# Twelve multiplications of the identity with itself in each token tile of a retention scan

## The chip, the cores and the metric

The kernel runs on one core of one Trainium2 chip. The metric is the device time of one execution, in microseconds (us).

## What is computed

Two layers of a backbone over 1024 latent and 256 context tokens. In each layer four mixers share an input and an output projection; then comes a ConvFFN. The mixer that matters here is the bidirectional retention, four heads of 64 channels, in chunks of 128 tokens:

```python
def step(s_mem, inp):
    qc, kc, vc = inp
    s = jnp.einsum('bhid,bhjd->bhij', qc, kc) * decay_mask
    o = jnp.einsum('bhij,bhjd->bhid', s, vc) + jnp.einsum('bhid,bhde->bhie', qc * q_dec[..., None], s_mem)
    s_new = s_mem * chunk_dec[:, None, None] + jnp.einsum('bhjd,bhje->bhde', kc * k_dec[..., None], vc)
    return s_new, o
```

The kernel folds both directions into one pass: the decay matrix `rD` holds the sum of the forward and the backward mask, and the state of a tile has the forward direction in its upper 64 rows and the backward in its lower 64.

## The kernel before

A layer runs in this order: input projections with the hyena mixer (`hyena`), the projections of mLSTM, retention and RWKV (`mlstm_proj`, `ret_proj`, `rwkv_front`), the retention itself (`retention`), then RWKV and mLSTM interleaved (`rwkv`, `mlstm`, with steps of the next modulation vectors), the output projection (L1042 to L1044 with `wo`), and the FFN. The time goes mostly to the big products of L1042 to L1044.

`retention` (L810) works on token tiles of 128: 10 in layer 0 (8 latent, 2 context) and 8 in layer 1. First it forms all tiles' key-value products (L840, out to `rSS` at L842) and runs the decay over them on GpSimd (L846, L847). Then comes the loop that the change touches, two nested functions:

- `load(t)` transposes q and k of the tile by TensorE (L852, four transposes into one PSUM bank) and copies them out by ScalarE (`rT`, L854); VectorE scales q by the decays (`q2`, L856), TensorE transposes that too (L858), ScalarE copies it out (L860; the trace names this tile rT as well).
- `use(t, ...)` makes the four heads' scores (L866; two heads share a bank, and even and odd heads lie in different halves of the partitions), VectorE multiplies them by the decay matrix into `rS` (L869, two halves), TensorE adds scores times values and decayed q times state (L872 and L873, one pair a head), and ScalarE copies the result over the tile's q (L874).

The loop calls `load(t+1)` before `use(t)`; after each second tile a group norm (L671 to L678) and a store to `yr` (L679) follow.

PSUM has eight banks: until the end of `retention` there are five `bank` and three `dbank`, each handed out in turn; a tile of `dbank` is given again once its last reader is done. `rwkv_front` uses dbanks in front of the scan (L422, read by VectorE at L423). Behind `retention` the function `psum` closes these pools and opens others on the same memory, and the RWKV stage's SBUF tiles take the room of the scan's.

The order of instructions on each engine isn't the program's: the whole kernel is built under a scheduler that simulates the times of the engines and writes each engine's stream in that order (`tile.TileContext(nc,schedule_with_timeline_sim=True)`). So work of neighbouring functions is mixed, and a change in one place can reorder others. Each engine then runs its stream strictly in turn.

Of the kernel before, what the change touches and what calls it, by code (L numbers as in the profile page):

```python
# [135 lines left out]
class Eng:  # L136

    def __init__(s,nc,pool): s.nc=nc; s.e=nc.gpsimd if pool else nc.vector; s.pool=pool
    def tt(s,out,a,b,op): s.e.tensor_tensor(out=out,in0=a,in1=b,op=op)
# [521 lines left out]
def tm(ap,nt):  # L661
    return ap[0:nt*128].rearrange("(t p) c -> p t c",p=128)


def group_norm(K,Y,out_y,nt,sqt,tag="gn",pool=None):

    nc=K.nc
    v=Y[:,0:nt]; h=Y.shape[2]; n=nt*h; th=lambda t: t[:,:n].rearrange("p (t h) -> p t h",h=h)
    q=sqt[:,:n].rearrange("p (t h) d -> p t h d",h=h)
    s,r=[th((pool or K.p_sm).tile([128,n],F32,tag=tag,name="gn_"+i,bufs=2)) for i in "sr"]  # L670
    nc.vector.tensor_reduce(out=s,in_=v,axis=mybir.AxisListType.X,op=ALU.add)  # L671
    nc.vector.tensor_scalar(out=s,in0=s,scalar1=1.0/64,scalar2=None,op0=ALU.mult)
    nc.vector.tensor_tensor(out=v,in0=v,in1=s.unsqueeze(3).to_broadcast([128,nt,h,64]),op=ALU.subtract)
    nc.scalar.activation(out=q,in_=v,func=ACTF.Square)
    nc.vector.tensor_reduce(out=r,in_=q,axis=mybir.AxisListType.X,op=ALU.add)
    nc.scalar.activation(out=r,in_=r,func=ACTF.Sqrt,scale=1.0/64,bias=K.eps5)
    nc.vector.reciprocal(out=r,in_=r)
    (nc.gpsimd if nt==2 else nc.vector).tensor_tensor(out=q,in0=v,in1=r.unsqueeze(3).to_broadcast([128,nt,h,64]),op=ALU.mult)  # L678
    nc.sync.dma_start(out_y,q.rearrange("p t h d -> p t (h d)"))  # L679


def mlstm(K,l,GT,last,side=None):
# [89 lines left out]
    def weights(t):  # L772
        iF,iB=FWT.index(t),BWT.index(t)
        S=p.tile([128,2,4,128],F32,tag="mI" if t%2==0 else "mL",name="S")
        for d in range(2):
            ru=RU[d]
            u_=U3[:,iF] if d==0 else U3[:,iB,::-1]
            nc.gpsimd.tensor_tensor(out=ru[32:40].rearrange("p (h i) -> p h i",h=4),in0=u_.unsqueeze(1).to_broadcast([8,4,128]),in1=C['mbd'][64:72,d].unsqueeze(2).to_broadcast([8,4,128]),op=A.mult)
            vo=VO[:,iF*128:iF*128+128] if d==0 else VOr[:,(9-iB)*128:(9-iB)*128+128]
            b=K.mbank()  # L780
            mm(b,vo,ru,start=True,stop=False)
            mm(b.rearrange("p (h i) -> p h i",h=4),identb,mmaskb[:,d].to_broadcast([128,4,128]),start=False,stop=True)
            act(out=S[:,d].rearrange("p h i -> p (h i)"),in_=b,func=ACTF.Exp)
        return [S[:,d] for d in range(2)]
    SN=weights(0)
# [30 lines left out]
def retention(K,l,last):  # L816
    nc=K.nc; p=K.p_rt; tt=nc.vector.tensor_tensor; act=nc.scalar.activation; mm=nc.tensor.matmul
    A=ALU; D=K.D
    C={n:p.tile(list(K.a['c_'+n].shape),F32,name="c"+n) for n in ('rD','rQD','rKD','rCD','rcos','rsin')}
    for n in C: nc.sync.dma_start(C[n],K.a['c_'+n])  # L820
    Q,KK_,V=[p.tile([128,10,256],F32,name="rqkv%d"%i) for i in range(3)]
    for i,X in enumerate((Q,KK_,V)):
        for t in range(8 if (last and i==0) else 10): nc.sync.dma_start(X[:,t],D['rqkv'][t*128:t*128+128,i*256:i*256+256])
    SS=p.tile([128,10,4,64],F32,name="rSS"); Y=Q.rearrange("p t (h d) -> p t h d",h=4)
    nc.gpsimd.memset(SS[0:64,FWT[0]],0.0); nc.gpsimd.memset(SS[64:128,BWT[0]],0.0)
    hv=lambda ap: ap.rearrange("p (h d) -> p h d",h=4)
    r5=lambda ap: ap.rearrange("p (h o s x) -> p h o s x",h=4,o=2,s=2)
    def rope(t):
        for X in (KK_,Q):
            x=X[:,t]; tmp=p.tile([128,256],F32,tag="rtmp",name="rtmp",bufs=3)  # L830
            for g in range(2):
                nc.gpsimd.tensor_tensor(out=r5(tmp)[:,:,:,g],in0=r5(x)[:,:,:,1-g],in1=C['rsin'][:,t].rearrange("p (o s x) -> p o s x",o=2,s=2)[:,:,g].unsqueeze(1).to_broadcast([128,4,2,16]),op=A.mult)
            tt(out=hv(x),in0=hv(x),in1=C['rcos'][:,t:t+1].to_broadcast([128,4,64]),op=A.mult)
            tt(out=x,in0=x,in1=tmp,op=A.add)
    for t in [8,9]+[0,7,1,6,2,5,3,4]:
        if t<8: rope(t)
        k2=p.tile([128,4,2,64],F32,tag="rq2",name="k2",bufs=4)
        tt(out=k2,in0=hv(KK_[:,t]).unsqueeze(2).to_broadcast([128,4,2,64]),in1=C['rKD'].unsqueeze(3).to_broadcast([128,4,2,64]),op=A.mult)
        b=K.bank()
        for h in range(4): mm(b[:,h*64:h*64+64],k2[:,h].rearrange("p a d -> p (a d)"),V[:,t,h*64:h*64+64],start=True,stop=True)  # L840
        for q,T in ((slice(0,64),FWT),(slice(64,128),BWT)):
            if t!=T[9]: act(out=SS[q,T[T.index(t)+1]].rearrange("p a d -> p (a d)"),in_=b[q,0:256],func=ACTF.Copy)  # L842
    for i in range(1,9):
        for q,T in ((slice(0,64),FWT),(slice(64,128),BWT)):
            cur,nx=T[i],T[i+1]; tmp=p.tile([128,4,64],F32,tag="rtmp",name="rst",bufs=3)
            nc.gpsimd.tensor_tensor(out=tmp[q],in0=SS[q,cur],in1=C['rCD'][q].unsqueeze(2).to_broadcast([64,4,64]),op=A.mult)  # L846
            nc.gpsimd.tensor_tensor(out=SS[q,nx],in0=SS[q,nx],in1=tmp[q],op=A.add)  # L847
    nt=8 if last else 10
    def load(t):
        b=K.bank()  # L850
        for i,X in enumerate((Q,KK_)):
            for f in range(2): nc.tensor.transpose(b[:,(i*2+f)*128:(i*2+f)*128+128],X[:,t,f*128:f*128+128],K.ident)  # L852
        T=p.tile([128,4,128],F32,tag="rT",name="rT",bufs=2)
        act(out=T.rearrange("p a b -> p (a b)"),in_=b,func=ACTF.Copy)  # L854
        q2=p.tile([128,4,2,64],F32,tag="rq2",name="q2",bufs=4)
        tt(out=q2,in0=hv(Q[:,t]).unsqueeze(2).to_broadcast([128,4,2,64]),in1=C['rQD'].unsqueeze(3).to_broadcast([128,4,2,64]),op=A.mult)  # L856
        b=K.bank()
        for h in range(4): nc.tensor.transpose(b[:,h*128:h*128+128],q2[:,h].rearrange("p a d -> p (a d)"),K.ident)  # L858
        T2=p.tile([128,4,128],F32,tag="rT2",name="rT2",bufs=2)
        act(out=T2.rearrange("p a b -> p (a b)"),in_=b,func=ACTF.Copy)  # L860
        return T,T2
    def use(t,T,T2):
        gr=[K.bank(),K.bank()]
        for h in range(4):
            p0=(h%2)*64; f=h//2
            mm(gr[h%2][:,f*128:f*128+128],T[p0:p0+64,2+f],T[p0:p0+64,f],start=True,stop=True)  # L866
        S=p.tile([128,4,128],F32,tag="rS",name="rS",bufs=2)
        Sv=S.rearrange("p (f q) i -> p f q i",q=2); Dv=C['rD'].rearrange("p (f q) i -> p f q i",q=2)
        for q in range(2): tt(out=Sv[:,:,q],in0=gr[q][:,0:256].rearrange("p (f i) -> p f i",f=2),in1=Dv[:,:,q],op=A.mult)  # L869
        b=K.bank()  # L870
        for h in range(4):
            mm(b[:,h*64:h*64+64],S[:,h],V[:,t,h*64:h*64+64],start=True,stop=False)  # L872
            mm(b[:,h*64:h*64+64],T2[:,h],SS[:,t,h],start=False,stop=True)  # L873
        act(out=Y[:,t].rearrange("p a d -> p (a d)"),in_=b[:,0:256],func=ACTF.Copy)  # L874
    nxt=load(0); done=0
    for t in range(nt):
        cur,nxt=nxt,load(t+1) if t+1<nt else None
        use(t,*cur)
        if t%2:
            sl=slice(done,t+1); done=t+1; n=sl.stop-sl.start  # L880
            group_norm(K,Y[:,sl],tm(D['yr'],nt)[:,sl],n,KK_[:,sl].rearrange("p t (h d) -> p (t h) d",h=4),"gnr",p)
# [587 lines left out]
```

## Time and profile before

| what | us |
|---|---|
| median of 3 runs | 4250.28 |
| lowest and highest of them | 4240.55, 4259.92 |
| the profiled execution | 4248.15 |
| its span, first to last instruction | 4246.4 |
| TensorE busy in the span | 3951.2 (93%) |
| VectorE busy | 2537.2 (60%) |
| ScalarE busy | 1413.6 (33%) |
| GpSimd busy | 764.7 (18%) |

The profile is of one execution, with 70484 instructions. PE is TensorE's matmul, PEld its weight load, DVE is VectorE, ACT ScalarE, POOL GpSimd, SP the engine that issues DMAs. The mean granted clock of TensorE was 0.946 of full speed; it has two levels, 1.0 (2.4 GHz) and 0.5 (1.2 GHz). Ends of matmuls are modelled, so a busy TensorE may still be one that waits.

### The profile page before, as it was taken

How to read it: one execution, taken by the hardware profiler on the slowest of the kernel's cores; microseconds unless marked ns; L12 is line 12 of the kernel's file. 1: busy time of each engine (PE TensorE's matmuls, PEld its weight loads, DVE VectorE, ACT ScalarE, POOL GpSimd, SP SyncE). 2: the span in 40 equal slices, each digit the busy share in tenths (PEclk: the TensorE clock that was granted, in tenths of full speed). 3: DMA queues.
4: the chain of work that ended last, by engine and by line, in shares of the span. 5: the costliest groups of instructions: out<-in, count | busy, mean ns of one | idle time of the engine just before them, and what ended most of it. 6: DMA issues, size and time to landing. Idle time of an engine off the chain costs nothing.

```text
span 4246.4 us, 70484 instructions
## 1 busy us (share of the span) xinstructions
PE 3951.2 (93%) x28176; PEld 3225.0 (76%) x28176; DVE 2537.2 (60%) x4756; ACT 1413.6 (33%) x2849; POOL 764.7 (18%) x1538
## 2 busy tenths in 40 slices
PE   5999999799979999999997999997899799999998
PEld 2788887677768888888885678886776678888886
DVE  5755665777669444444448565677767684444447
ACT  4433333554344211111113433344543442212121
POOL 3320023323312000000021221025432220000002
PEclk6999999799989999999998999998898799999999
DMA  4235554344443110111103325554333331111112
GB/s 165 76 96 180 151 156 121 109 149 125 129 147 120 46 40 30 45 40 35 35 30 121 90 87 157 171 162 118 118 115 109 124 111 55 50 40 55 45 50 99
DMA packets 477154, 414.50 MB, mean 98 GB/s; under 512 B 48827, under 2 KB 443284, under 8 KB 474010
## 3 DMA queue, kind: packets, MB, share of 16 engines
q1 hardware_dynamic: 476826, 409.99, 31.1%
q8 instruction: 222, 3.64, 0.3%
q14 instruction: 106, 0.87, 0.1%
HBM read 323.65 MB, written 86.25 MB: 97 GB/s over the span
## 4 chain that ended last, share of the span: by engine, by line
PE 53%; DVE 9%; DMA 4%; issue 2%; ACT 2%; POOL 1%; SPq 1%; DVEq 0%; ACTq 0%; POOLq 0%
PE bank L1043 9%; PE bank L1042 9%; PE bank L1044 9%; PE dbank L1042 6%; PE dbank L1043 6%; PE dbank L1044 6%; DVE bst L1003 1%; DMA xt<-x 1%; DVE facc L1225 1%; PE mbank L993 1%; PE bank L186 1%; DMA adaw<-in_ada_w 1%; PE bank L187 1%; DVE facc L1226 0%; DMA wst<-in_w_out 0%
## 5 line engine op out<-in xcount | busy, mean ns | idle before, releaser
L1042 PE MATMUL dbank<-uh,wh 128*128 128x512 f32 (+1 forms) x2120 | 763.7, 369 | 8.6 <-ACT tmpB L398 5.5
L1043 PE MATMUL dbank<-ul,wh 128*128 128x512 f32 (+1 forms) x2120 | 759.8, 367 | 0.0
L1036 DVE TENSOR_TENSOR wl<-wst,wh 128x1024 fp32r<-128x1024 f32 x146 | 185.9, 1275 | 510.3 <-ACT wh L1035 355.1
L1044 PE MATMUL dbank<-uh,wl 128*128 128x512 f32 (+1 forms) x2120 | 481.5, 367 | 0.0
L1042 PEld LDWEIGHTS dbank<-uh,wh 128*128 128x128 f32 x2120 | 400.6, 189 | 84.0 <-ACT tmpB L398 5.9
L1043 PEld LDWEIGHTS dbank<-ul,wh 128*128 128x128 f32 x2120 | 400.9, 189 | 68.7 <-issue 1.1
L1044 PEld LDWEIGHTS dbank<-uh,wl 128*128 128x128 f32 x2120 | 365.7, 188 | 71.0 <-issue 1.7
L1284 DVE TENSOR_TENSOR facc<-facc,bank 128x512 f32<-128x512 f32 x324 | 221.8, 687 | 205.1 <-PE bank L1044 205.1
L1042 PE MATMUL bank<-uh,wh 128*128 128x512 f32 (+1 forms) x920 | 334.9, 372 | 4.5 <-ACT uh L1030 4.5
L1043 PE MATMUL bank<-ul,wh 128*128 128x512 f32 (+1 forms) x920 | 335.1, 372 | 0.8 <-DVE ul L1031 0.8
L1042 PE MATMUL bank<-wdh,gh 128*128 128x512 f32 x792 | 315.6, 400 | 15.7 <-DVE facc L1298 5.7
L1043 PE MATMUL bank<-wdl,gh 128*128 128x512 f32 x792 | 310.4, 392 | 1.0 <-DVE wdl L1036 1.0
L1253 POOL MEMSET fz<- 128x1 f32 x132 | 7.3, 99 | 1433.4 <-DVE fc L1268 1213.5
L1044 PE MATMUL bank<-wdh,gl 128*128 128x512 f32 x792 | 247.7, 391 | 0.0
L1035 ACT ACTIVATE wh<-wst 128x1024 fp32r<-128x1024 f32 x146 | 154.7, 1060 | 237.5 <-PE dbank L1043 164.5
L1035 ACT ACTIVATE wdh<-wst 128x1024 fp32r<-128x1024 f32 x46 | 48.8, 1062 | 523.7 <-PE bank L1044 431.4
L1044 PE MATMUL bank<-uh,wl 128*128 128x512 f32 (+1 forms) x920 | 211.9, 372 | 0.0
L1042 PEld LDWEIGHTS bank<-uh,wh 128*128 128x128 f32 x920 | 174.1, 190 | 36.1 <-ACT uh L1030 5.6
L1043 PEld LDWEIGHTS bank<-ul,wh 128*128 128x128 f32 x920 | 174.2, 189 | 31.9 <-DVE ul L1031 1.7
L1042 PEld LDWEIGHTS bank<-wdh,gh 128*128 128x128 f32 x792 | 149.7, 189 | 56.9 <-DVE facc L1298 11.0
L1044 PEld LDWEIGHTS bank<-uh,wl 128*128 128x128 f32 x920 | 161.5, 188 | 33.1
L1043 PEld LDWEIGHTS bank<-wdl,gh 128*128 128x128 f32 x792 | 149.7, 189 | 34.6 <-issue 3.2
(490 smaller groups left out, 7856.9 us busy)
## 6 DMA issues: line engine op xcount, KB each, us to landing
wst<-in_ffn_w_up SPq DMA_DIRECT2D x88, 512.0 KB
adaw<-in_ada_w SPq DMA_DIRECT2D x160, 256.0 KB
wst<-in_w_in SPq DMA_DIRECT2D x58, 512.0 KB
wst<-in_ffn_w_down SPq DMA_DIRECT2D x46, 512.0 KB
df<-in_c_F SPq DMA_DIRECT2D x10, 1344.0 KB
xt<-x SPq DMA_DIRECT2D x26, 512.0 KB
df<-in_c_I SPq DMA_DIRECT2D x8, 1344.0 KB
rkk<-wrk SPq DMA_DIRECT2D x10, 1024.0 KB
```

What stands on the lines that cost most here:

```text
L186: mm(dst_re,F[:,i],pre(slot),start=True,stop=False); mm(dst_re,F[:,i+1],pim(slot),start=False,stop=True)
L187: mm(dst_im,F[:,i],qim(slot),start=True,stop=False); mm(dst_im,F[:,i+2],qre(slot),start=False,stop=True)
L993: for j in range(2): nc.tensor.matmul(ps[32*j:32*j+2,0:128],k.sc[:,q],w[u][q//2][:,q%2,j*128:j*128+128],start=(q==0),stop=(q==7))
L1003: for h in range(2): nc.vector.bn_stats(out=st[:,h],in_=x[h])
L1035: k.nc.scalar.activation(out=h,in_=st,func=ACTF.Copy)
L1036: k.nc.vector.tensor_tensor(out=lo,in0=st,in1=h,op=ALU.subtract)
L1042: mm(ps,lh,rh,start=(i==0),stop=False)
L1043: mm(ps,lh,rl,start=False,stop=False)
L1044: for i,((lh,ll),(rh,rl)) in enumerate(pairs): mm(ps,ll,rh,start=False,stop=(i==n-1 and more is None))
L1225: for o,i,gg in zip([y[:,h] for h in hs],x,[g[:,h] for h in hs]) if parts else [(y,x,g)]: stt(out=o,in0=i,scalar=m,in1=gg,op0=ALU.subtract ...
L1253: for q in (0,1025,1282): nc.gpsimd.memset(z[:,q:q+1],0.0)
L1284: else: tt(out=d,in0=d,in1=ps,op=ALU.add)
```

## The change

Before the loop one more dbank is taken and named `idle`. A function `turn(n)` multiplies the identity with itself n times into its first 128 columns, each time with start and stop set. It is called with 4 at three places: at the end of `load`, after the scores, and after the products with values and state. Nothing reads the bank.

```diff
     nt=8 if last else 10
+    idle=K.dbank()
+    def turn(n):
+        for _ in range(n): mm(idle[:,0:128],K.ident,K.ident,start=True,stop=True)
     def load(t):
         b=K.bank()
...
         act(out=T2.rearrange("p a b -> p (a b)"),in_=b,func=ACTF.Copy)
+        turn(4)
         return T,T2
     def use(t,T,T2):
         gr=[K.bank(),K.bank()]
         for h in range(4):
             p0=(h%2)*64; f=h//2
             mm(gr[h%2][:,f*128:f*128+128],T[p0:p0+64,2+f],T[p0:p0+64,f],start=True,stop=True)
+        turn(4)
         S=p.tile([128,4,128],F32,tag="rS",name="rS",bufs=2)
...
             mm(b[:,h*64:h*64+64],T2[:,h],SS[:,t,h],start=False,stop=True)
+        turn(4)
         act(out=Y[:,t].rearrange("p a d -> p (a d)"),in_=b[:,0:256],func=ACTF.Copy)
```

In the changed kernel the added matmul is L851; L852 has become L855, L858 L861, L866 L870, L872 L877 and L873 L878.

The scheduler places the added matmuls by its own times. Where they begin in layer 0, TensorE's order before was this (the last pairs of tile 1, then half of tile 2's scores, L866):

```order
L873 MATMUL bank<-rSS,rT_6289 128x64
L866 MATMUL bank<-rT 128x128 x2
L872 MATMUL bank<-rqkv_6025,rS 128x64
L873 MATMUL bank<-rSS,rT_6340 128x64
L852 MATMUL bank<-ident,rqkv_6023 128x128 x2
L852 MATMUL bank<-ident,rqkv_6024 128x128 x2
```

And this is the same place now:

```order
L878 MATMUL bank<-rSS,rT_6290 128x64
L870 MATMUL bank<-rT 128x128
L851 MATMUL dbank<-ident 128x128 x32
L870 MATMUL bank<-rT 128x128
L851 MATMUL dbank<-ident 128x128 x4
L877 MATMUL bank<-rqkv_6025,rS 128x64
L878 MATMUL bank<-rSS,rT_6357 128x64
L851 MATMUL dbank<-ident 128x128 x4
```

A burst of 32, those that had been asked for since tile 0, stands between two of tile 2's scores.

A settled tile of layer 0 on TensorE before, from one pair of scores to the next (the L872 and L873 behind the second pair come twice more):

```order
L866 MATMUL bank<-rT 128x128 x2
L872 MATMUL bank<-rqkv_6025,rS 128x64
L873 MATMUL bank<-rSS,rT_6502 128x64
L852 MATMUL bank<-ident,rqkv_6023 128x128 x2
L852 MATMUL bank<-ident,rqkv_6024 128x128 x2
L858 MATMUL bank<-ident,q_6576 128x128 x4
L866 MATMUL bank<-rT 128x128 x2
L872 MATMUL bank<-rqkv_6025,rS 128x64
L873 MATMUL bank<-rSS,rT_6502 128x64
```

And now, from the transposes to the first of four L877, L878:

```order
L855 MATMUL bank<-ident,rqkv_6023 128x128 x2
L855 MATMUL bank<-ident,rqkv_6024 128x128 x2
L861 MATMUL bank<-ident,q_6618 128x128 x4
L851 MATMUL dbank<-ident 128x128
L870 MATMUL bank<-rT 128x128 x4
L851 MATMUL dbank<-ident 128x128 x13
L877 MATMUL bank<-rqkv_6025,rS 128x64
L878 MATMUL bank<-rSS,rT_6567 128x64
```

The four scores of a tile stand together, and the added matmuls stand between them and the products that use them.

In layer 1 the first added matmuls on TensorE stand behind the last two L422 (the products of `rwkv_front` with `bones`):

```order
L870 MATMUL bank<-rT 128x128 x4
L422 MATMUL dbank<-tmpA,bones 128x512 x2
L851 MATMUL dbank<-ident 128x128 x24
L877 MATMUL bank<-rqkv_25219,rS 128x64
L851 MATMUL dbank<-ident 128x128 x4
```

Before, the L872 followed the L422 directly.

## Rows read from the trace of the kernel before

**Rows 1.** The page, busy time, share of the span and instructions of each engine.

```profile
PE 3951.2 (93%) x28176; PEld 3225.0 (76%) x28176; DVE 2537.2 (60%) x4756; ACT 1413.6 (33%) x2849; POOL 764.7 (18%) x1538
```

**Rows 2.** Windows over the settled scans: stretch, length; busy us (instructions) by engine; clock; DMA.

```profile
735.70:766.90 31.20, 31.20 (x241) 27.55 (x240) 16.94 (x39) 14.63 (x30) 3.38 (x3) 1.00 0.13 48
2904.40:2932.20 27.80, 27.49 (x217) 24.46 (x215) 14.41 (x31) 12.24 (x25) 5.54 (x6) 1.00 0.11 39
```

**Rows 3.** The chain that ended last, layer 1: start us, us, engine, tile, line, count.

```profile
2900.32 3.78 PE dbank L422 x4
...
2904.99 0.61 ACT rT L854
...
2924.06 0.44 PE bank L852 x4
...
2924.94 0.64 PE bank L866 x4
2925.58 0.36 PE bank L872 x2
2925.95 0.22 PE bank L873 x2
...
2928.29 0.65 PE bank L866 x8
...
2932.24 0.39 ACT rqkv L874
...
2937.57 2.12 DMA yr<-rqkv
```

**Rows 4.** Waits after layer 0's scan: who waited for whom, us, times, longest.

```profile
ACT lw L491 <- DMA yr<-rqkv: 3.7, 1, 3.7
DVE identb L691 <- DMA yr<-rqkv: 3.4, 1, 3.4
```

**Rows 5.** Chain at the inverse transform of layer 1; then the instructions of L852.

```profile
2774.45 3.14 PE bank L219 x28
...
L852 PE MATMUL bank<-ident,rqkv x72: 272/273/421, 712.1 to 2924.2; 128*128 128x128 f32 x72
```

**Rows 6.** Timeline of VectorE in the last tiles of layer 1: start us, us, what.

```profile
2928.96 0.42 DVE L869 TENSOR_TENSOR rS<-bank,crD 128x256 f32<-128x256 f32 x1 [0.35 <-PE bank L866]
...
2929.90 0.42 DVE L869 TENSOR_TENSOR rS<-bank,crD 128x256 f32<-128x256 f32 x1
```

**Rows 7.** Timeline of layer 0's scan where it settles.

```profile
730.32 3.52 PE L422 MATMUL dbank<-tmpA,bones 128*128 128x512 f32 x4
...
734.12 1.62 DVE L423 TENSOR_TENSOR tmpB<-dbank,tmpB 128x512 f32<-128x512 f32 x3 [3.56 <-DMA tmpB<-wvf]
...
735.71 0.71 PE L866 MATMUL bank<-rT 64*128 64x128 f32 x4
```

**Rows 8.** Windows over the stretches of low clock at the two scans.

```profile
723.30:733.50 10.20, 7.40 (x22) 5.38 (x23) 2.67 (x3) 0.87 (x2) 6.80 (x8) 0.50 0.47 128
...
771.10:781.30 10.20, 4.09 (x28) 3.18 (x30) 3.11 (x7) 5.68 (x10) 7.36 (x19) 0.50 0.64 189
2887.30:2894.10 6.80, 5.72 (x28) 5.39 (x30) 6.80 (x10) 2.85 (x6) 6.42 (x8) 0.50 0.51 172
2897.60:2904.40 6.80, 5.52 (x17) 2.96 (x16) 3.50 (x5) 0.43 (x1) 6.25 (x8) 0.50 0.24 77
...
2935.20:2948.70 13.50, 6.23 (x43) 4.61 (x44) 5.80 (x12) 8.12 (x15) 8.11 (x21) 0.50 0.59 167
```

**Rows 9.** Windows over the start of each scan's loop, ahead of the settled part.

```profile
712.00:735.70 23.70, 15.93 (x95) 12.62 (x93) 14.41 (x24) 4.89 (x10) 17.60 (x21) 0.78 0.41 125
2889.90:2904.00 14.10, 10.93 (x51) 7.82 (x51) 9.88 (x13) 3.74 (x7) 12.97 (x16) 0.62 0.55 158
```

**Rows 10.** Windows over the RWKV and mLSTM stage of each layer.

```profile
767.00:1210.00 443.00, 393.55 (x6173) 304.84 (x6173) 312.01 (x797) 202.06 (x547) 143.76 (x384) 0.90 0.41 126
2932.00:3400.00 468.00, 396.11 (x5845) 311.88 (x5845) 326.13 (x801) 217.13 (x588) 154.15 (x384) 0.85 0.40 123
```

## The prediction, made before the changed kernel had run

> **What bounds the kernel now.** I read the page first: TensorE is busy 93% of a span of 4246.4 us, more than any other engine [rows 1]. That share is an average, so the second view is the table of windows over the two stretches in which the retention scan has settled: 31.20 of 31.20 us busy in layer 0 and 27.49 of 27.80 us in layer 1, with the granted clock at 1.00 (its 2.4 GHz level), while VectorE and ScalarE stand near half [rows 2]. Busy could still hide waits, since ends of matmuls are modelled, so the third view is the chain of what ended last. From the end of the L422 at 2904.10 to ScalarE's copy at 2932.24 us of layer 1 it is TensorE almost without a break (one pause of 0.6 us at 2904.99 for rT); one period of one token tile, from the L852 at 2924.06 to the L866 at 2928.29, takes 4.23 us [rows 3]. Behind the last L873 come that copy, the group norm, and the store of yr, which starts at 2937.57. The fourth view, the waits after the scan, shows that the RWKV stage's first work on ScalarE and VectorE is released by that store (3.7 and 3.4 us waited in layer 0) [rows 4]. So work put on TensorE inside the scan is on the path: scan, group norm, store, next stage.
>
> **The change, part by part.**
>
> *The added matmuls.* The program text has 12 a tile, 10 tiles in layer 0 and 8 in layer 1: 216, and the order written out holds them all (120 and 96). Price: 14 plain f32 matmuls of 128x128 by 128 columns (7 slots, two at L219) are 28 records of 3.14 us together, so a matmul is two records of 0.112 us each at clock 1.00 [rows 5]. A transpose of the same size is one record: L852 is called 72 times and recorded 72 times [rows 5]. The added instructions are plain matmuls, not transposes, though the identity is an operand: two records. 432 x 0.112 = 48.4 us, 26.9 in layer 0 and 21.5 in layer 1. The lower bound of the price is the transpose's one record, 24.2 us; I take the upper end since L219 has the same shape, type and form.
>
> The Trainium skill (TensorE: Matmul & The Clock Gate, section Back-to-back issue gap) gives about 81 ns for a sustained matmul of 128 columns; by it the added work would be an estimated 17.5 us and the total about 4258 us. The trace has 0.112 us a record and two records a matmul in this type, and the measurement decides.
>
> *What the new order gives back.* Before, in 7 tiles of layer 0 and 5 of layer 1, the four L866 products of a tile stand in two pairs, with the previous tile's products between them. A pair takes 0.64 us, and the first L872 after it 0.36 us where the others take 0.22; all four in one group take 0.65 us [rows 3]. So each tile whose two groups become one saves 0.64 + 0.36 - 0.22 - 0.01 = 0.77 us. In the changed order 6 tiles of layer 0 and all 5 of layer 1 become whole: 11 x 0.77 = 8.5 us back. One tile of layer 0 (row 1991) is cut into three pieces by the burst; I charge half of 0.77, 0.4 us. A settled tile goes from 4.23 to 4.23 - 0.77 + 24 x 0.112 = 6.15 us.
>
> *Does the new order stall?* L872 needs rS, which VectorE makes behind L866: after the L866 group of 2928.29 the two halves ended at 2929.38 and 2930.32, about 2.0 us behind its start, with a group norm step between them [rows 6]. Now 11 to 14 added matmuls stand between the L866 group and L872: 0.65 + 22 x 0.112 = 3.1 us. Covered. Only the last tile has just two there (0.45 us); even so the first L872 needs only the first half, about 1.1 us behind the start, and there the group itself and the two give 1.1. I cost that at nothing; if the cover fails it is at most the missing second half, 0.9 us a layer. ScalarE and VectorE have half their time free in the scan [rows 2] and get 6.15 us for the same work.
>
> *The PSUM bank.* `idle` takes one of three dbanks, so its first matmul waits for VectorE's L423 on an earlier tile. In layer 0 that ended at 735.74, as the L866 began before which the burst of 32 now stands [rows 7]; in layer 1 it was long done. Cost nothing. The bank's memory then goes to the next stage; the one early use there, two L706 products, moves from mid-scan to its end (0.5 us on the same engine, only moved).
>
> *The clock.* Five low stretches at 0.50 (the 1.2 GHz level) lie around the scans, with TensorE busy 7.40, 4.09, 5.72, 5.52 and 6.23 us in them [rows 8]; before each the engine had waited. The new matmuls can't shorten these: the bursts stand behind L422 in the order, that is behind 733.5 and 2904.1, when the clock is back or about to be, and the waits after the scan (group norm, store) hold none of them. Term 0.
>
> *Downstream.* The scheduler, which works from simulated times, also writes the RWKV and mLSTM stages in another order (some 600 of the 13,245 TensorE rows). No row prices that. TensorE is unoccupied 49.5 of 443 us and 71.9 of 468 us there [rows 10]; I let the reordering win or lose a tenth of that, 12 us, as an estimate, and take 0.
>
> Sum: 26.9 - 4.6 + 0.4 = 22.7 us in layer 0, 21.5 - 3.9 = 17.6 in layer 1, together 40.3. The profiled execution took 4248.15 us, 2.1 below the median of the three runs, 4250.28. 4248.15 + 40.3 = 4288.5; I say 4289, 0.9% up on either base. Three runs spread over 19 us, 0.46%, so about 0.5% (21 us) is what a measurement can tell from no change.
>
> **Rivals.**
>
> A: not slower, by a warm and free filler. If the matmuls ran in TensorE's waits ahead of the settled scan and kept the clock at 1.00 through the five stretches, half of their 28.96 us of busy time would come back, 14.5 us: 4234. It decides by whether they stand ahead of the L422 at 2900.32 [rows 3] and 730.32 [rows 7]; the order puts them behind. And the unoccupied time there is 7.8 + 3.2 = 11 us against 48 [rows 9]. Chance 3%.
>
> The Trainium skill (TensorE: Matmul & The Clock Gate, section HAM oscillation) says that gaps between bursts of matmuls throttle the array, and that keeping it busy keeps it fast. The trace agrees on the cause, not on the place: the settled scan is already at 1.00, and no gap is filled.
>
> B: one record a matmul, the price of the transposes: 24.2 - 8.5 + 0.4 = 16.1, so 4264. For it only that an identity is an operand. Chance 5%.
>
> C: dearer. The give-back doesn't come (48.4), and the reordered stages lose 12: 4309. For it: order from simulated times owes the chip nothing; against: the L866 rows are exact to 0.01 us. Chance 13%.
>
> D: the reordering downstream pays 20 us or more, so that 4268 or less is left, by filling a sixth of TensorE's gaps there [rows 10]. Chance 7%.
>
> E: the change doesn't do what it says, the matmuls being dropped as dead: 4248. They stand in the order. Chance 2%.
>
> **How the numbers follow.** My forecast, 70%, spans 40.3 with 12 either way: 4277 to 4301. Leaving out A, E and the far ends of C and D, the range for 8 in 10 is 4266 to 4308; B lies just under it. Over 0.5% faster needs the extreme of D: 2%. Within 0.5%, under 4271: A, B, E and most of D, 14%. Slower: the rest, 84%.
>
> **What would show it.** In the changed profile the group dbank<-ident at L851 should count 432 matmuls of about 275 ns with no idle before them and 0.112 us apart in the chain; a settled tile should take 6.15 us; the last L878 (L873 before) should come 22.7 us later in layer 0; L870 (L866 before) should mostly stand in groups of eight records; the clock in the scan should stay 1.00 and the low stretches after both scans should remain. I am wrong if L851 counts 216, if idle time opens at L877 behind rS (the cover failed), or if the stretch from the end of a scan to L1042 on wo has changed by over 12 us: then the scheduler's ripple, not the added work, decides.

## The result, and the profile after

The changed kernel takes 4308.16 us (median of 4 runs, 4299.04 to 4326.61) against 4253.66 for the kernel before, run beside it (4 runs): ratio 1.0138, 95% interval 1.0108 to 1.0169. It is slower by 1.4%; forecast were 0.9% and 4266 to 4308 us, so the median lies just above the range. The profiled execution took 4311.25 us (span 4309.4), 63 us more than that of before. The ratios here and below leave out three executions of 4846 us and more, one each of the experiments e3 and f6 and of the kernel before.

The page of the changed kernel, busy time by engine, against [rows 1]; then its groups by line, the added one:

```profile
PE 4002.4 (93%) x28608; PEld 3270.9 (76%) x28608; DVE 2534.6 (59%) x4756; ACT 1417.2 (33%) x2851; POOL 767.4 (18%) x1538
```

```profile
L851 PE MATMUL dbank<-ident 128*128 128x128 f32 x432 | 54.4, 280 | 0.0
```

TensorE has 432 records more, all of them L851, two for each of 216 matmuls, with no idle time ahead of them. Next are the settled scans in the windows view [rows 2], then the chain that ended last through one tile of layer 1 [rows 3]; the columns are as there:

```profile
743.00:787.00 44.00, 44.00 (x400) 41.81 (x398) 13.49 (x31) 12.18 (x25) 3.13 (x3) 1.00 0.06 19
2970.00:3006.00 36.00, 36.00 (x327) 34.12 (x326) 11.99 (x28) 11.54 (x24) 3.13 (x3) 1.00 0.07 23
```

```profile
2983.27 0.44 PE bank L855 x4
2983.71 0.44 PE bank L861 x4
2984.15 0.22 PE dbank L851 x2
2984.37 0.65 PE bank L870 x8
2985.01 3.10 PE dbank L851 x26
2988.11 0.17 PE bank L877 x2
2988.28 0.22 PE bank L878 x2
...
2989.85 0.44 PE bank L855 x4
```

The scan is TensorE without a break at clock 1.00. The four scores stand whole (0.65 us), the added matmuls behind them. This tile holds 28 added records and takes 6.58 us; the four settled tiles of layer 1 take, from the last L878 of one to that of the next, 5.59, 6.58, 5.91 and 6.58 us, on average 6.17.

Where the 63 us come from is read from windows over four stretches: each layer's scan (from the last state product L840 to the last L873, now L878), and the RWKV and mLSTM stage behind it (to the last L650). Before:

```profile
711.95:766.70 54.75, 46.98 (x335) 40.09 (x334) 31.27 (x62) 19.52 (x40) 21.02 (x24) 0.91 0.25 81
767.20:1185.10 417.90, 372.11 (x6039) 287.38 (x6040) 298.83 (x763) 194.43 (x537) 141.59 (x383) 0.91 0.42 131
2889.90:2931.90 42.00, 38.52 (x266) 32.51 (x266) 24.52 (x43) 15.98 (x32) 18.88 (x22) 0.87 0.25 79
2932.50:3360.00 427.50, 361.23 (x5685) 283.05 (x5685) 303.61 (x761) 202.10 (x562) 140.84 (x378) 0.85 0.38 118
```

The changed kernel:

```profile
708.40:786.76 78.36, 72.29 (x574) 65.85 (x574) 32.06 (x62) 20.15 (x40) 21.87 (x25) 0.89 0.19 61
787.30:1239.00 451.70, 389.60 (x6038) 296.83 (x6038) 303.75 (x761) 197.07 (x539) 143.19 (x382) 0.87 0.39 121
2944.80:3005.90 61.10, 56.48 (x459) 51.59 (x458) 24.74 (x44) 16.32 (x32) 20.01 (x23) 0.90 0.19 59
3006.40:3426.60 420.20, 356.27 (x5685) 278.92 (x5685) 298.96 (x761) 201.50 (x562) 140.82 (x377) 0.86 0.39 120
```

The scans grew by 23.6 and 19.1 us (22.7 and 17.6 were forecast). Layer 0's stage, in which nothing was added (6039 and 6038 matmul records), grew by 33.8, half as busy time at a lower clock (372.11 to 389.60 us, 0.91 to 0.87), half as time in which TensorE is unoccupied (45.8 to 62.1). Layer 1's stage lost 7.3. That makes 69 us; the rest of the execution took 6 us less. The test that the prediction set itself answers too: the first L1042 on wo (now L1048) stands 466.9 us behind layer 0's scan before and 498.2 us behind it now, 31 us more, over its 12.

The waits of TensorE in layer 0's stage, of before and then of the changed kernel (who waited for whom; us, times, longest):

```profile
PE pbank L496 <- ACT ex L501: 17.4, 2, 8.8
PE mbank L993 <- DMA adaw<-in_ada_w: 9.9, 11, 3.6
PE dbank L544 <- DVE G L534: 5.9, 2, 5.6
```

```profile
PE mbank L999 <- DMA adaw<-in_ada_w: 16.0, 13, 2.9
PE dbank L544 <- DVE G L534: 11.3, 3, 6.2
PE pbank L496 <- ACT ex L501: 8.8, 2, 8.6
PE mbank L731 <- ACT me L727: 6.3, 1, 6.3
```

A new wait of 6.3 us (L731, the decays of mLSTM) and longer ones for the conditioning weights (adaw) and VectorE look like the culprits (that of L496 became shorter). The experiments say otherwise about the first.

### The profile page after: what moved, and what is told of

The parts are those of the page before. It is cut to its first block, busy times and chain, and to the rows that moved or that the text cites. A ratio compares the mean times of both kernels' runs of the same rounds, so it can differ in the third digit from the quotient of the medians.

```text
span 4309.4 us, 71341 instructions
## 1 busy us (share of the span) xinstructions
PE 4002.4 (93%) x28608; PEld 3270.9 (76%) x28608; DVE 2534.6 (59%) x4756; ACT 1417.2 (33%) x2851; POOL 767.4 (18%) x1538
## 5 line engine op out<-in xcount | busy, mean ns | idle before, releaser
L1048 PE MATMUL dbank<-uh,wh 128*128 128x512 f32 (+1 forms) x2120 | 763.3, 369 | 8.6 <-ACT tmpB L398 5.5
L1042 DVE TENSOR_TENSOR wl<-wst,wh 128x1024 fp32r<-128x1024 f32 x146 | 185.9, 1274 | 488.8 <-ACT wh L1041 364.3
L1048 PEld LDWEIGHTS dbank<-uh,wh 128*128 128x128 f32 x2120 | 400.3, 189 | 84.3 <-ACT tmpB L398 5.9
L1048 PE MATMUL bank<-uh,wh 128*128 128x512 f32 (+1 forms) x920 | 334.8, 372 | 3.8 <-ACT uh L1036 3.8
L1048 PE MATMUL bank<-wdh,gh 128*128 128x512 f32 x792 | 315.0, 400 | 16.7 <-DVE facc L1304 7.0
L1048 PEld LDWEIGHTS bank<-uh,wh 128*128 128x128 f32 x920 | 174.2, 190 | 35.1 <-ACT uh L1036 4.4
L1048 PEld LDWEIGHTS bank<-wdh,gh 128*128 128x128 f32 x792 | 149.6, 189 | 59.0 <-DVE facc L1304 13.8
L1087 ACT ACTIVATE z<-dbank 128x512 f32<-128x512 f32 (+1 forms) x160 | 85.6, 535 | 275.0 <-PE dbank L1050 262.7
```

Of the source, the lines that this page charges most:

```text
L1042: k.nc.vector.tensor_tensor(out=lo,in0=st,in1=h,op=ALU.subtract)
L1048: mm(ps,lh,rh,start=(i==0),stop=False)
L1087: nc.scalar.activation(out=z[:,oo:oo+n],in_=b[:,:n],func=ACTF.Copy)
```

## The experiments

Three theories stood at the start for the missing term. O: the planner (the scheduler that writes the order), whose simulated times the added matmuls shift, wrote a worse order behind the scan. G and M: the order is innocent, and the granted clock there falls otherwise from run to run (G), or lower behind the added work (M). To tell them apart the order had to be held. All runs but n2 call this at the end of `tile_backbone`; ORDER holds, for each engine, the numbers of the instructions in the order of another kernel, and each is tied behind the one before it, in issue order alone, without a semaphore:

```diff
+    in_order(nc,tc)
     close_u(k); k.psum_es.close()
...
+def in_order(nc,tc):
+    import zlib,base64,json
+    traced={i.name:i for i in nc.cur_bb.bb.instructions}
+    for queue in json.loads(zlib.decompress(base64.b85decode(ORDER))):
+        n,prev=0,None
+        for d in queue:
+            n+=d; i=traced.get("I-%d"%n)
+            if i is None: continue
+            if prev is not None: tc.add_manual_dep(i,prev.name,mybir.DependencyInfo(mybir.DependencyClass.NoSync,mybir.DependencyReason.DATA),reason="order")
+            prev=i
```

Measured (stretches as above, from the start of the first mark to the start of the last; "busy" is TensorE's in layer 0's stage, us, with its granted clock; the ratio is to the kernel before in the same session, the stretches are of the one profiled execution):

| run | ratio, 95% | scan 0 | stage 0 | busy, clock | scan 1 | stage 1 |
|---|---|---|---|---|---|---|
| before | 1 | 54.7 | 418.1 | 372.1, 0.91 | 42.0 | 427.8 |
| the change | 1.0138 (1.0108-1.0169) | 78.4 | 452.0 | 389.6, 0.87 | 61.1 | 420.5 |
| e1 | 1.0089 (1.0059-1.0119) | 76.8 | 414.7 | 368.2, 0.92 | 62.1 | 421.3 |
| e2 | 1.0056 (1.0033-1.0079) | 54.2 | 439.0 | 379.5, 0.89 | 43.3 | 426.8 |
| e3 | 1.0028 (1.0005-1.0051) | 65.3 | 425.4 | 379.4, 0.88 | 45.7 | 417.1 |
| e4 | 1.0203 (1.0169-1.0236) | 102.2 | 423.9 | 373.5, 0.91 | 79.5 | 421.5 |
| f1 | 1.0001 (0.9987-1.0016) | 54.2 | 417.3 | 368.9, 0.91 | 45.5 | 420.3 |
| f7 | 1.0022 (1.0006-1.0038) | 54.6 | 425.1 | 374.2, 0.90 | 63.6 | 415.2 |
| f6 | 1.0015 (1.0006-1.0025) | 54.8 | 428.5 | 373.7, 0.90 | 44.4 | 424.0 |
| f4 | 1.0074 (1.0049-1.0098) | 54.4 | 441.1 | 384.5, 0.87 | 58.9 | 423.8 |
| f2 | 1.0043 (1.0028-1.0058) | 54.6 | 441.3 | 384.7, 0.87 | 44.9 | 420.8 |
| f5 | 1.0044 (1.0030-1.0058) | 54.2 | 439.1 | 378.0, 0.89 | 64.3 | 414.8 |
| f3 | 1.0053 (1.0027-1.0079) | 54.4 | 450.0 | 388.5, 0.87 | 44.0 | 425.3 |
| n2 | 1.0067 (1.0045-1.0090) | 65.6 | 437.1 | 379.4, 0.89 | 53.8 | 429.4 |
| g1 | 1.0031 (1.0016-1.0045) | 64.3 | 421.0 | 369.4, 0.91 | 51.5 | 432.5 |

**The scan and the order, apart.** e1 is the changed kernel with ORDER from the kernel before for everything behind each scan; e2 is the kernel before with ORDER from the changed kernel there.

> The changed kernel's retention scan, its 216 added matmuls in the same places, with every instruction written behind the scan held in the order that the kernel before has, engine by engine. Theory O (the order that the planner wrote behind the scan is what was missed): only the scan's own growth is left, 23.6 us in layer 0 and 19.0 in layer 1 by the traces of before and after, so 4253.7 + 42.6 = 4296 us, ratio 1.010; layer 0's stretch from the last L878 (before: L873) to the last L650 takes 418 us as in the kernel before, not 452. Theory G (the order is innocent; the granted clock in that stretch falls otherwise from run to run): the stretch is anything from 415 to 455 us, and the ratio stays near 1.014. Theory M (the added matmuls leave TensorE granted less clock in the stretch behind them): the stretch is 450 us here too, and the time 4308, ratio 1.0138.

> The reverse: the kernel before, its scan untouched and nothing added, with every instruction behind the scan held in the order that the changed kernel has. Theory O: what the order alone costs, 54.5 - 42.6 = 12 us by the medians to 63.0 - 42.6 = 20 us by the two profiled executions: 4266 to 4274 us, ratio 1.003 to 1.005, with layer 0's stretch behind the scan at 452 us and layer 1's at 420. Theories G and M: 4254 us, ratio 1.000, layer 0's stretch at 418 (M) or anywhere between (G).

e1 costs 0.89% and e2 0.56%; multiplied they give 1.0145, the change's 1.0138 within its interval. Layer 0's stage, e1 and then e2:

```profile
785.95:1200.67 414.72, 368.22 (x6040) 284.15 (x6039) 298.14 (x762) 194.08 (x537) 140.25 (x381) 0.92 0.43 132
```

```profile
768.00:1207.02 439.02, 379.45 (x6039) 290.96 (x6039) 302.03 (x762) 196.84 (x539) 143.59 (x382) 0.89 0.41 124
```

With the order of before the stage takes 415 us behind 216 added matmuls; with the order of the change it takes 439 behind none. Theory O holds, G and M fall: about 38 us of 4244 (the base of that session) are the scan's, 24 the order's. e2's stage missed its figure: 452 us were expected, the change's. In the same order it is 13 us shorter, mostly as busy time (379.5 for 389.6 us) at a higher clock (0.89 for 0.87); these are one execution each, and what made that difference isn't shown. Layer 1's stage doesn't follow its order (421 us in e1 with that of before, 427 in e2 with that of the change).

**Twice as many, half as long.** e4 is e1 with `turn(8)` for each `turn(4)`; g1 is e1 with this:

```diff
-        for _ in range(n): mm(idle[:,0:128],K.ident,K.ident,start=True,stop=True)
+        for _ in range(n): nc.tensor.transpose(idle[:,0:128],K.ident,K.ident)
```

> Eight matmuls at each call instead of four, 432 in all, everything behind the scan in the order of before. If each costs its two records and nothing hides it, 216 more add 216 x 0.224 = 48.4 us to the run with four: 4253.7 + 42.6 + 48.4 = 4345 us, ratio 1.0214, settled tile 6.15 + 12 x 0.224 = 8.84 us. If part of the first four lay in the idle time of the tile and the give-back is no such thing, the next four cost the same 48.4 all the same; if a longer group runs cheaper or dearer, the settled tile shows it. Theory M: the stretch behind layer 0's scan grows again, beyond 452 us; theory O: 418.

> The changed kernel with each added matmul written as a transpose of the identity, in the same 216 places, the scan in the changed kernel's order, all behind it in the order of before; the transposes of L852 leave one record of 112 ns each in the trace of before, the float32 matmuls two. If the price of the addition is its records (the prediction's 432 x 0.112 us), 216 records of 0.112 us take away 24.2 us against the run with matmuls in the same frame: settled tile 6.25 - 12 x 0.112 = 4.90 us, scan of layer 0 from 76.8 to 63.4 us, of layer 1 from 62.1 to 51.4 us, ratio 1.0089 - 0.0057 = 1.0032. If a filler's price is a slot in the order and not its records, the tile stays at 6.25 us. A little of the saving may be lost, up to 0.3 us a tile, where eleven short ones no longer cover the 1.2 us that L872 waits for L869 without fillers.

e4 measured 1.0203 for 1.0214. Its settled tiles, measured as those of the change, alternate between 9.08 and 8.64 us, 8.86 on average for 8.84. The scans grew by 25.4 and 17.3 us over e1, for 26.9 and 21.5; layer 1's scan ran at a granted clock of 0.93 for 0.88 in e1, which is an estimated 2 of the 4 us missing there, and the rest stays open. g1 measured 1.0031 for 1.0032; L851 counts 216 records, the scans are 64.3 and 51.5 us for 63.4 and 51.4. The price of the added work is its records, as the prediction had it. Neither moves stage 0 out of 415 to 425 us.

**The give-back.** e3 is the kernel before with ORDER from the changed kernel inside the scans and its own behind them.

> The kernel before with no matmul added: the scan's instructions stand in the order of the changed kernel (the four products of L866 in one group, where two groups of two stood), everything behind it in the order of before. If the prediction's give-back is real (0.77 us in each of 11 tiles), the settled tile falls from 4.23 to 3.46 us and the time by 8.5 us, to 4245, ratio 0.998. If the added matmuls are dearer or cheaper than 0.224 us and no give-back exists, the tile stays at 4.23 and the ratio at 1.000.

Both expectations failed: the scans became longer, 65.3 and 45.7 us. What TensorE's L872 waited in layer 0's scan, in the kernel before and in e3, then a window over e3's scan:

```profile
PE bank L872 <- DVE rS L869: 4.7, 2, 2.5
```

```profile
PE bank L872 <- DVE rS L869: 11.7, 10, 2.8
```

```profile
734.00:776.00 42.00, 34.17 (x249) 30.50 (x248) 17.11 (x38) 15.08 (x31) 4.17 (x4) 0.82 0.12 42
```

With the scores whole and nothing behind them, L872 waits for VectorE's product with the decay mask ten times in 66 us, twice in the kernel before, and the clock falls to 0.82 in a scan that held 1.00. In the kernel before, the previous tile's products cover that time; in the changed kernel the added matmuls do. So the give-back is real, but belongs to cover and order together.

**Where the order loses.** These are the kernel before with nothing added. Layer 0's 15,898 instructions behind the scan stand up to a border in one kernel's order, behind it in the other's. Borders are key transposes of mLSTM's state pass (L753): f1 has the change's order for 382 instructions, f7 for 840, f6 for 1038, f4 for 1715, f2 for 2709; f3 has the order of before for 402 and then the change's, f5 for 1543. f5 to f7 also hold both scans in the order of before; layer 1 behind its scan has that order in all seven.

> The kernel before, nothing added. Behind layer 0's scan the first 382 instructions (up to the first key transpose of mLSTM's state pass, L753) stand in the changed kernel's order, all behind them and layer 1 in the order of before. Since the order alone was seen to cost 23.6 us, this asks where. Theory O1 (it is lost at once, in the gates ahead of the state pass, where the changed kernel's order shows a new wait of L731 for the activation L727 of 6.3 us): about +6 to +20 us, ratio 1.0015 to 1.005, layer 0's stretch 425 to 440 us. Theory O2 (it is lost in how the state pass and the RWKV chunks are interleaved after that): ratio 1.000, the stretch at 415 to 425 us as in the three executions seen with the order of before.

> As the run before, but the changed kernel's order reaches to the end of mLSTM's state pass (2709 instructions). Theory O1: the same as the run before. Theory O2: here the state pass falls behind by the 20 to 30 us that the trace of the reversed case shows between 876 and 968 us, and if the chunks' lead is what pays, the stretch grows to 435 to 445 us, ratio 1.004 to 1.006. Theory O3 (it is lost in the second half, where mLSTM's outputs and the last RWKV chunks run): still 1.000, 415 to 425 us.

> The other side: layer 0's first 402 instructions behind the scan in the order of before, all others up to layer 1's scan in the changed kernel's order. Theory O1: ratio 1.000, stretch 415 to 425 us. Theories O2 and O3: most of the order's cost, ratio 1.004 to 1.006, stretch 435 to 450 us.

> The kernel before, nothing added; the changed kernel's order from layer 0's scan to the middle of mLSTM's state pass (1715 instructions), the order of before behind that. The whole state pass in that order made the stretch 441 us, its first 382 instructions 417 us. If the loss grows along the pass (many places of the interleaving, each a little), about half of the 23 us shows: 425 to 433 us, ratio 1.002 to 1.003. If it is one place, the stretch is either 415 to 420 us or 438 to 444 us.

> The kernel before, nothing added, both scans held in their own order; layer 0's instructions behind the scan in the order of before up to the middle of mLSTM's state pass (1543 instructions), from there to layer 1's scan in the changed kernel's order. If the loss is made in the first half of the pass alone, the stretch is 415 to 425 us and the ratio 1.000. If any part in the changed kernel's order loses (the planner's later choices are as bad), 430 to 445 us, ratio 1.003 to 1.006.

> As above with the two orders exchanged and the border earlier: the changed kernel's order to the ninth key transpose (1038 instructions, two steps of each direction), the order of before behind it. If the loss of 23 us sits ahead of the border, the stretch is 438 to 444 us, ratio 1.004 to 1.006; if behind it, 415 to 425 us and 1.000; between, if several places share it.

> The same with the border at the fifth key transpose (840 instructions; 382 of them cost nothing). If the loss is made between 840 and 1038 instructions, 415 to 425 us here and ratio 1.000; if between 382 and 840, where the second RWKV chunk's products and the first conditioning product change places, 438 to 444 us, ratio 1.004 to 1.006.

f1 carries the suspected wait, and no cost of it shows (ratio 1.0001, by its interval at most 1.0016; stage 417 us for 418):

```profile
PE mbank L731 <- ACT me L727: 6.3, 1, 6.3
```

Theory O1, 6 to 20 us at this place, falls (by the ratio all but its lowest end, and the stage shows none of it): what this wait holds up isn't what ends late. f1 also holds the order of every engine behind both scans, so holding an order costs nothing that shows. Moving the border on, the stage takes 417, 425, 429, 441 and 441 us. The profiled executions with the order of before lie between 415 and 425, so f7's 425 shows no loss, and its ratio of 1.0022 may come from layer 1's scan, which took 63.6 us in the profiled execution. f6 loses a little (by its ratio 6 us, 1.0006 to 1.0025), f4's stage all of it: the loss isn't one place but grows over the first half of the state pass, mostly behind f6's border, where the RWKV chunks and the mLSTM steps are interleaved. And it isn't only there: with the first half from before and the rest from the change, f5's stage loses 21 us again (f4 and f5, too, had a longer scan of layer 1 in their profiled executions, so their ratios are not the stage's alone). The two halves don't add up (f4 23, f5 21, the whole 21 in e2 and 34 in the change). What f1 and f2 show in the same slices of that pass (first f1, then f2):

```profile
860.00:880.00 20.00, 18.68 (x407) 15.16 (x407) 15.08 (x43) 11.38 (x40) 6.78 (x21) 0.99 0.49 157
920.00:940.00 20.00, 18.41 (x340) 14.62 (x340) 13.39 (x42) 6.10 (x26) 12.61 (x43) 0.95 0.34 100
```

```profile
860.00:880.00 20.00, 20.00 (x404) 16.93 (x402) 11.98 (x40) 7.11 (x31) 8.23 (x28) 0.76 0.20 56
920.00:940.00 20.00, 18.33 (x187) 12.63 (x182) 9.80 (x27) 9.01 (x25) 7.83 (x28) 0.57 0.28 84
```

TensorE is as busy, but at 0.76 and 0.57 of its clock. Over the stage, TensorE is unoccupied for 46 to 52 us with the order of before (before, f1, e1, e3, e4, g1) and granted 0.88 to 0.92; for 57 to 62 us in f2, f3, f4, f5, e2 and the change, and granted 0.87 to 0.89. f6 and f7 lie between (55 and 51 us, 0.90). More pauses and a lower clock mostly come together; e3, with 46.0 us and 0.88, is an exception. The Trainium skill (TensorE: Matmul & The Clock Gate, section HAM oscillation) says that pauses between bursts throttle the array; these rows agree, except for e3. No run here was made to change one without the other, so that the pauses bring the clock down is argued, not shown.

**Another size, the planner free.** n2 is the changed kernel with `turn(2)`, no order held.

> Two matmuls at each call instead of four, 108 in all, and the planner free to write its own order everywhere. The scan alone should grow by about half of what 216 gave, by 42.6 / 2 = 21 us, ratio 1.005, if every matmul costs its 0.224 us wherever it stands; it grows by less, 5 to 15 us, if it takes a group of eleven in front of L872 to fill a wait that a shorter one leaves open (then waits of L872 for L869 show). Theory O: layer 0's stretch behind the scan is written anew, and takes any length between 415 and 452 us, another one than that of before or of the change; a planner that is innocent leaves it at 418 us.

The scans grew by 10.8 and 11.8 us, 22.6 for the forecast 21, and stage 0 came out at 437.1: half the added work, another written order, another loss of 19 us in that stage. But the planner rewrote the work ahead of the scan as well, which here began 7.7 us earlier, and the whole ratio leaves about 6 us beyond the scans' 22.6 (-4 to 16 by its interval). So a loss of n2's order as a whole isn't shown.

**A version that beats both.** g3 puts useful work where the added matmuls stood. `use` is split, and TensorE's instructions are pinned in the order in which they are written:

```diff
-    def use(t,T,T2):
+    def scores(t,T):
...
+    def products(t,b,S,T2,heads):
...
+    cur=load(0); S=scores(0,cur[0]); done=0
+    for t in range(nt):
+        nxt=load(t+1) if t+1<nt else None
+        b=K.bank(); products(t,b,S,cur[1],range(3)); S0=S
+        if nxt: S=scores(t+1,nxt[0])
+        products(t,b,S0,cur[1],[3]); cur=nxt
...
-        use(t,*cur)
```

h2 pins from the fourth tile on (against g3; each pinned instruction also passes its t):

```diff
-    pin=K.tc.keep_in_program_order
+    pin=lambda t,i: K.tc.keep_in_program_order(i) if t>2 else i
```

> The kernel before with nothing added, its scan's TensorE instructions in one fixed order in every tile: the four score products of L866 whole, then the previous tile's last head, the next tile's eight transposes, three heads of this tile; all behind the scan in the order of before. What the added matmuls did in the changed kernel, stand in the 1.2 us between L866 and L872 while VectorE multiplies, useful work does here. If the give-back is real and only wants cover, the settled tile falls from 4.23 to 3.5 to 3.7 us, both scans together by 8 to 10 us, ratio 0.998. If the transposes come too late for ScalarE's copy in front of the next L866, the wait moves there (L866 for rT L854) and the tile stays at 4.2 us or above, ratio 1.000 or more.

> As the run that put useful work into the wait for L869, but the first three tiles are left to the planner, so that they run ahead while POOL still builds the states (L847); the fixed order holds from the fourth tile on; all behind the scan in the order of before. That run's settled tile was 3.40 us against 4.23, but its scans began late (no tile ahead of the states) and gave it back: 54.5 and 49.7 us against 54.7 and 42.0. If the start was all that ate the gain, seven tiles of layer 0 and five of layer 1 now keep 0.8 us each: scans of 49 to 50 and 38 to 39 us, together 8 to 9 us less, ratio 0.998. If the stretch behind the scan waits for something else than the scan's end (VectorE or POOL in front of L496), that gain is taken back there and the ratio is 1.000.

g3: ratio 1.0003 (0.9989 to 1.0017). The chain through one of its tiles in layer 1 (L867 are the scores, L874 and L875 the products, L853 and L859 the transposes):

```profile
2925.66 0.65 PE bank L867 x8
2926.31 0.36 PE bank L874 x2
2926.67 0.22 PE bank L875 x2
2926.89 0.45 PE bank L853 x4
2927.34 0.44 PE bank L859 x4
2927.78 0.17 PE bank L874 x2
...
2929.06 0.65 PE bank L867 x8
```

3.40 us a tile where before took 4.23, but with no tile ahead of the states the scans took 54.5 and 49.7 us: the gain went into the start. h2, which lets the first tiles run ahead, took 4237.05 us against 4245.71: ratio 0.9975, interval 0.9961 to 0.9989. Layer 0's scan is 50.5 us, 4.2 less, about as expected. Layer 1's, at 47.9, is 5.9 us longer, where 38 to 39 were expected. There L874 waits 3.1 us for its rS, behind VectorE's group norm (L872 waited 1.9 before), and a stretch that ran at a clock of 1.00 before [rows 2] ran at 0.59:

```profile
2905.00:2920.00 15.00, 13.05 (x65) 12.39 (x66) 5.74 (x12) 4.93 (x9) 5.37 (x7) 0.59 0.09 36
```

So that h2 beats the kernel before is measured, but its one profile, of the slowest of its twelve executions, doesn't show where the 9 us come from: what layer 0's scan gains, layer 1's loses.

## Why the prediction was right and where it failed

- *The bound* held: TensorE is the path in the scan, and work added there is paid in full.
- *The price of the added matmuls*, 432 records of 0.112 us, held: 216 instead of 432 records took 0.58% off (g1), 432 more put 1.14% on (e4). The lower bound, one record, belongs to a transpose. By the gap that the Trainium skill gives (TensorE: Matmul & The Clock Gate, section Back-to-back issue gap, 81 ns) it would have been an estimated 17.5 us; the scans grew by 42.7 with the give-back already taken off, and that decides against it.
- *The give-back* held in size inside the changed kernel: settled tiles of 6.17 us on average for 6.15. As worded, that whole groups of scores save 0.77 us, it was half the reason: e3 has the whole groups and loses.
- *No stall, no wait for the bank, no clock term* held in the scan (1.00, no idle time before L851). With them the scans' sum, 40.3 us forecast, was 42.7 in the profiles and 0.89% of 4244, 38 us, in e1.
- *Downstream* is the step that failed: taken at 0, with 12 us either way as an estimate. It measured 24 us (e2, 0.33 to 0.79%). Two things were wrong in how it was sized. A tenth of TensorE's unoccupied time is no bound on what another order does: that time grew by about a third (46.0 to 59.6 us in e2, 62.3 in the change). And it left out the rest of the loss, busy time at a lower clock (7.4 us in e2, 17.5 in the change), because the clock was looked at around the scans alone. Why this order brings more pauses and less clock stays open.
- *The rivals*: C's number, 4309, is close to the result by luck: the give-back that it left out came, and the order behind cost twice its 12 us. A, B, D and E fell.

## What to carry to other kernels

An edit whose own cost is sure can still move every instruction behind it when a planner sets the order from simulated times; hold the order of the rest, measure the two apart, and give the reordering a range from other orders of the same stage (here its profiles ran from 415 to 452 us), not from its idle time. Before blaming a new wait in a trace, put the order that makes it into the old kernel: here a wait of 6.3 us showed no cost. And where a filler seems to help, ask what it covers: with useful work in the same place a tile took 3.40 us, with the filler 6.17.

## What was not expected of the hardware

In the profiled executions of f4, f5 and f7, layer 1's scan ran at half clock through stretches of 28 us and more in which TensorE had no pause; of f7:

```profile
2916.00:2930.00 14.00, 14.00 (x61) 12.76 (x60) 3.79 (x9) 5.37 (x10) 1.40 (x2) 0.50 0.15 57
2930.00:2945.00 15.00, 15.00 (x64) 13.43 (x63) 3.46 (x8) 3.34 (x8) 0.00 (x0) 0.50 0.00 1
```

A tile took 7.80 us there instead of 4.23 and the scan 63.6 us instead of 42 to 46, though f5 and f7 have that scan in the order of before. The Trainium skill (TensorE: Matmul & The Clock Gate, section Why this matters for your kernels) says that a TensorE kept busy comes to full speed; here 29 us of unbroken work did not bring it there, and the measurement decides. That it isn't in every execution is argued from the times: f7's ten ran from 4240 to 4268 us and the profiled one was the second slowest. So one profile can be some 20 us off in such a place, and the ratios, not the stretches, carry the verdicts above.
